# A seventh group by block products, and the residual added later: one transformer layer on one core

## The chip, the cores and the metric

The kernel runs on one core of a Trainium2 chip. The metric is device time in microseconds (us) for one execution. The core's engines each work through a queue of their own, in order: TensorE (PE; its weight loads stand apart as PEld), VectorE (DVE), ScalarE (ACT), GpSimd (POOL) and SyncE (SP). SP, POOL and ACT also issue transfers between device memory and the on-chip buffer (SBUF); matmul results land in eight PSUM banks.

## The reference

One decoder layer over 512 tokens with model width 2048, all in fp32:

```
h = x + gla_mixer(rmsnorm(x) * norm_mix) @ w_out          # gated linear attention, 4 heads
h = h + square(relu(rmsnorm(h) * norm_mlp @ w_up)) @ w_down   # 2048 -> 8192 -> 2048
gate = sigmoid(rmsnorm(h) * norm_ple @ w_ple_gate)        # 2048 -> 2048
h = h + gate * (p @ w_ple_proj)                           # p: 512 x 256
out = rmsnorm(h) * norm_final
```

The change lies in the product with `w_down`, in how the residual `h` is joined to it, and in the gate behind it.

## The kernel before, in words

Every matmul of weights is done three times: a helper splits each fp32 operand into a rounded high part and the low rest, and hi·hi, hi·lo and lo·hi are summed in PSUM (`mm3`, L148). ACT makes the high part, DVE the low part by a subtraction.

Activations lie transposed: 128 rows of features by 512 tokens. The token-wise scale of the MLP's norm is taken out of the matmuls. The hidden layer is computed from unscaled values; since relu squared of f·v is f²·relu²(v), the output of `w_down` lacks the factor F2 = f² of each token. So the residual is multiplied by 1/F2 (the tile `g2`) before the MLP's sum is added to it, and the whole by F2 at the end. Both factors are made in `rest_of_scale` (L818): a row of 4 values per partition is spread over a 128x512 tile by a matmul (`bcast`, L219).

`w_up` and `w_down` are worked in chunks: 512 rows of the weights by 256 columns. There are two ways for a chunk.

- *Block products* (`chunk`, L843). The 256x256 blocks with the two halves of the tokens form 2x2 block matrices, multiplied by seven products instead of eight (a Strassen scheme: `PRODUCTS`, L738). A chunk is 2 times 7 products times 3 = 42 matmuls of 256 columns. It needs sums of weight blocks, made by DVE in `chunk_sums` (L741: one instruction of 128x512, two of 128x256), two high parts of 128x896 on ACT (L846) and two low parts on DVE (L848); and sums of the activations' blocks (the operands `d`). At the end of a group of chunks `combine` (L860) adds the seven results from four PSUM banks into a tile `e` of the single buffer `w`, by one ACT copy and five DVE instructions.
- *Plain* (`plain_chunk`, L917): 24 matmuls of 512 columns, with one high part on ACT (L140) and one low part on DVE (L142), 128x1024 each. Two PSUM banks. There is nothing to combine.

The up product has 32 groups (g) of 4 chunks, all by block products. Its results go to device memory, as blocks (`z_d`) and as differences of blocks (`zd_d`). The down product has 8 groups of 256 output columns and 16 chunks of 512 rows, which are cut into five slices of 3, 3, 3, 3 and 4 chunks (`SLICES`, L34), since only a slice's hidden activations fit in SBUF. Within a slice all 8 groups run; groups in `PLAIN` = (0, 7) take the plain way, the other six block products. Slice 0 runs its groups in the order 0, 7, 1 to 6 (L761), the others in order.

After each group in each slice the partial result is added to the running residual: `residual_in` (L887) loads `h_d[g]` (512 KB), and in slice 0 multiplies it by `g2` (L891); DVE adds two times 128x512 (L903 or L927); `residual_out` (L894) writes it back, in slice 4 after a multiplication by F2 (L896). `late` work like this is queued in `todo` and run after the second chunk of the next group. While a slice runs, the hidden activations of the next are loaded and split (`build_to` and `build_sums_to`: `split`, L909, a POOL load, an ACT cast L913, a DVE subtraction L914, 128x1024 each), into 34 shared slots that come free as the old slice's chunks are used up.

Two smaller pieces lie between: `embedding` (L958) transposes `p`, in slice 0 after group 1; `project_embedding` (L971) multiplies it by a quarter of `w_ple_proj`, 24 matmuls of 512 columns into four PSUM banks, four ACT copies into two tiles, and two stores of 512 KB to `pp_d`; it follows group 7 in slices 1 to 3 and group 6 in slice 0. The gate stage behind (L1101) loads the finished residual, makes its squares' sums for the norm (`r3`, L1116), multiplies by `w_ple_gate` and ends in `finish` (L1091).

The order in which each engine's queue gets its instructions is made by a planner when the program is built: it goes through the program's order as priorities, with the times that it expects, and hands out buffers. An instruction whose data it expects later can be passed by others. At run time the queues are fixed.

Of the kernel before, what the change touches and what calls it, by code (L numbers as in the profile page):

```python
# [9 lines left out]
F32 = mybir.dt.float32  # L10
# [6 lines left out]
P = 128  # L17
# [16 lines left out]
SLICES = (3, 3, 3, 3, 4)  # L34
PLAIN = (0, 7)

# [24 lines left out]
def trunk_kernel(ctx, tc, a, out):  # L61
# [723 lines left out]
    def evac_out(i, ps):  # L785
        kp = i // 2
        if i % 2 == 0:
            late["x"] = (load2 if kp == 5 else load)([P, 2, T], f"xres_{kp}")
            nc.gpsimd.dma_start(late["x"], xT_d[i:i + 2].rearrange("k p t -> p k t"))
            if kp in (5, 6):  # L790
                late["u"] = late["x"]
            else:
                late["w"] = wide(f"u_{kp}")
                late["u"] = late["w"][:, 0:4, :].rearrange("p (a h) t -> p a (h t)", a=2)
            late[kp] = late["u"]
        h = late["x"][:, i % 2, :]
        nc.vector.tensor_tensor(out=h, in0=ps, in1=h, op=ALU.add)
        add_squares(h, f"mlp_{i}", i == 0)
        if kp not in (5, 6):
            scale_out(i, h)  # L800
        if i % 2:
            nc.gpsimd.dma_start(h_d[kp], late["x"])
            if kp in (5, 6):
                for j in range(2):
                    scale_out(i - 1 + j, late["x"][:, j, :])
            if i == 13:
                first_raw.append(raw_of(0))
            if kp < 5:
                XOPS[kp] = operands(kp, late["u"], late["w"][:, 4:8, :], "X")
# [4 lines left out]

    F2 = []
    g2 = mpool.tile([P, T], F32, tag="g2", name="g2")

    def rest_of_scale():  # L818
# [5 lines left out]
        nc.vector.tensor_tensor(out=f, in0=r, in1=rinv, op=ALU.mult)  # L824
        ft = tiny([P, NTT], "ft")
        nc.vector.tensor_tensor(out=ft, in0=f, in1=f, op=ALU.mult)
        F2.append(mpool.tile([P, T], F32, tag="acc2", name="f2"))
        bcast(ft, F2[0], "f2")
        gi_ = tiny([P, NTT], "gi")
# [56 lines left out]

    def residual_in(s_, g):  # L887
        hs = (load2 if g % 3 == 2 else load)([P, 2, T], f"h_{s_}_{g}")
        nc.gpsimd.dma_start(hs, h_d[g])
        if s_ == 0:  # L890
            nc.vector.tensor_tensor(out=hs, in0=hs, in1=g2.unsqueeze(1).broadcast_to([P, 2, T]), op=ALU.mult)  # L891
        return hs

    def residual_out(s_, g, hs):  # L894
        if s_ == len(SLICES) - 1:
            nc.vector.tensor_tensor(out=hs, in0=hs, in1=F2[0].unsqueeze(1).broadcast_to([P, 2, T]), op=ALU.mult)  # L896
        nc.gpsimd.dma_start(h_d[g], hs)

    def add_slice(s_, g, ps):
        _, z = combine(ps, f"dn{s_}_{g}")  # L900
        hs = residual_in(s_, g)
        for f in range(2):
            nc.vector.tensor_tensor(out=hs[:, f, :], in0=hs[:, f, :], in1=z[:, 1 - f, :], op=ALU.add)  # L903
        residual_out(s_, g, hs)

# [17 lines left out]

    def add_plain(s_, g, ps):
        hs = residual_in(s_, g)
        for i in range(2):
            nc.vector.tensor_tensor(out=hs[:, i, :], in0=hs[:, i, :], in1=ps[i], op=ALU.add)  # L927
        residual_out(s_, g, hs)
    built = [0, 0]
# [41 lines left out]
    def project_embedding(gi):  # L971
        hi, lo = load_w(w_rows(w_pp, 0, 2, 512 * gi, 512), [P, 2, 512], f"wp{gi}")
        for t2 in range(NTT // 2):
            o = (load2 if (2 * gi + t2) % 3 == 2 else load)([P, 2, 512], f"pp_{gi}_{t2}")
            for t in range(2):
                ts_ = slice((2 * t2 + t) * P, (2 * t2 + t + 1) * P)
                ps = bank(f"ps_ple{gi}_{t2}_{t}")
                for k in range(2):
                    mm3(ps, (PT[k][:, 0, ts_], PT[k][:, 1, ts_]), (hi[:, k, :], lo[:, k, :]), k == 0, k == 1)
                nc.scalar.copy(o[:, t, :], ps)  # L980
            nc.scalar.dma_start(
                pp_d[2 * t2:2 * t2 + 2, :, 512 * gi:512 * gi + 512].rearrange("t p c -> p t c"), o)

    raw_next = first_raw[0]
    ps = None
    for n, (stage, g, k4, first, last) in enumerate(work):
        raw, raw_next = raw_next, raw_of(n + 1)
        s_ = stage - 1
        if stage == 0:
# [6 lines left out]
            if g == 0 and k4 == 2:  # L996
                rest_of_scale()
        else:
            end = sum(SLICES[:stage])
            if g == 0:  # L1000
                build_to(k4 + 1)
# [3 lines left out]
            if g in PLAIN:  # L1005
                if first:
                    ps = [bank(f"ps_{name}_{i}") for i in range(2)]
                plain_chunk(ps, k4, g, first, last, f"{name}_{k4}")
                if s_ == 0 and g == 0:
                    flush()  # L1010
                    build_to(min(k4 + 2, end))
                if s_ == 0 and g == 7:
                    build_sums_to(k4 + 1)
            else:
                if first:
                    ps = group_banks(g % 2 == 0, name)
                chunk(ps, raw, k4, ZOPS, first, last, f"{name}_{k4}")
            if last and end < NG // 2:
                if g == 1 and not s_:
                    embedding()  # L1020
                if g == 2 and SLICES[s_] == 3:
                    build_to(end + 2)
                if g == 6:
                    build_to(end + 3)
                if g == (7 if s_ else 6):
                    project_embedding(s_)
                    build_sums_to(end + 1)
        if todo and not first:
            todo.pop(0)()
        if last:  # L1030
            if stage == 0:
                ze = []
                todo.append(lambda g=g, ps=ps, ze=ze: ze.append(hidden(g, ps)))
                todo.append(lambda g=g, ze=ze: hidden_sums(g, *ze))
            else:
                todo.append(lambda s_=s_, g=g, ps=ps: (add_plain if g in PLAIN else add_slice)(s_, g, ps))
    flush()
# [53 lines left out]
    def finish(t, gi, psg, pp, ph):  # L1091
# [4 lines left out]
        d = hn[t][c0 // 1024][:, c0 % 1024:c0 % 1024 + w]  # L1096
        nc.vector.tensor_tensor(out=d, in0=sg[:, :w], in1=ph, op=ALU.add)
        nc.scalar.activation(out=sg[:, :w], in_=d, func=AF.Square, accum_out=ssf[:, t, gi:gi + 1])
        nc.vector.tensor_tensor(out=d, in0=d, in1=nf[c0 // 1024][:, c0 % 1024:c0 % 1024 + w], op=ALU.mult)

    for gi, (c0, w) in enumerate(GROUPS):  # L1101
        nk = 1024 // w
        if gi < len(GROUPS) - 1:
# [61 lines left out]
```

## Time and profile before

| | |
|---|---|
| median of 3 runs | 2371.59 us (2369.11 to 2375.26) |
| the profiled execution | 2369.4 us, its span 2367.6 us |
| PE busy | 2331.3 us, 98% of the span |
| PEld busy | 2129.9 us, 90% |
| DVE busy | 1731.8 us, 73% |
| ACT busy | 987.2 us, 42% |
| POOL busy | 186.7 us, 8% |
| granted TensorE clock, mean | 0.997 |

The span runs from the first to the last instruction of the profiled execution. Shares are means over all stages: DVE's 73% hides that it is lighter in the gate and the mixer and heavier in the MLP. The down product lies between 1469.9 and 2170.2 us of the span, the gate stage behind it.

### The profile page before, as it was taken

The page shows a single profiled execution, that of the slowest core. Times are in us where ns is not written, and L with a number is a line of the kernel's source. Part 1 is how long each engine was busy: PE and PEld are TensorE (multiplying, and loading weights), DVE is VectorE, ACT ScalarE, POOL GpSimd, SP SyncE. Part 2 cuts the span into 40 slices and gives each one's busy share as a digit, 9 for nine tenths or more (in the row PEclk, how much of TensorE's full clock was granted, in tenths as well). Part 3 has the DMA queues.
Part 4 walks back from the last instruction along what each step waited for, and adds up shares of the span by engine and source line. Part 5 has one row for each costly group of instructions (what it writes and reads, how often), then busy time and mean ns, then how long its engine had stood idle before and what let it go on. Part 6 is the DMA issues. An engine that isn't in the chain of part 4 may idle for free.

```text
span 2367.6 us, 37470 instructions
## 1 busy us (share of the span) xinstructions
PE 2331.3 (98%) x15066; PEld 2129.9 (90%) x15066; DVE 1731.8 (73%) x2700; ACT 987.2 (42%) x1237; POOL 186.7 (8%) x346
## 2 busy tenths in 40 slices
PE   8999999999999999999999999999999999999998
PEld 7888888888888899999999999898989898998887
DVE  6664737447555698988898887798979687898435
ACT  5433323324333345444444444444443444335233
POOL 3000000000100000000000001101010101101000
PEclk9999999999999999999999999999999999999999
DMA  8322323232434345545554446647575757646433
GB/s 277 106 81 89 89 81 104 84 98 85 135 128 151 118 157 163 167 154 160 161 159 154 158 151 216 219 161 273 191 263 176 276 169 258 198 160 216 119 114 113
DMA packets 256975, 374.73 MB, mean 158 GB/s; under 512 B 14756, under 2 KB 203360, under 8 KB 256800
## 3 DMA queue, kind: packets, MB, share of 16 engines
q1 hardware_dynamic: 213072, 228.68, 31.6%
q0 software_dynamic: 39456, 139.31, 16.4%
q10 hardware_dynamic: 4272, 4.33, 0.6%
q8 instruction: 118, 1.93, 0.3%
q14 instruction: 57, 0.47, 0.1%
HBM read 297.83 MB, written 74.45 MB: 157 GB/s over the span
## 4 chain that ended last, share of the span: by engine, by line
PE 85%; DMA 5%; DVE 4%; issue 2%; ACT 1%; POOL 0%; ACTq 0%; DVEq 0%; POOLq 0%
PE ps_up L857 8%; PE ps_up L856 8%; PE ps_up L854 8%; PE ps_d L857 5%; PE ps_d L854 5%; PE ps_d L856 5%; PE ps_v L150 2%; PE ps_wo L150 2%; PE ps_wo L151 2%; PE ps_v L151 2%; PE ps_og L150 2%; PE ps_og L151 2%; PE ps_v L152 2%; PE ps_og L152 2%; PE ps_wo L152 2%
## 5 line engine op out<-in xcount | busy, mean ns | idle before, releaser
L846 ACT CAST whi_up<-raw_up 128x896 fp32r<-128x896 f32 x256 | 238.3, 940 | 299.0 <-PE ps_up L856 255.6
L848 DVE TENSOR_TENSOR wlo_up<-raw_up,whi_up 128x896 fp32r<-128x896 f32 x256 | 277.3, 1086 | 43.8 <-ACT whi_up L846 43.8
L854 PE MATMUL ps_up<-XS,whi_up 128*128 128x256 f32 x1024 | 290.1, 283 | 0.0
L857 PE MATMUL ps_up<-XS,wlo_up 128*128 128x256 f32 x1024 | 290.0, 283 | 0.0
L856 PE MATMUL ps_up<-XS,whi_up 128*128 128x256 f32 x1024 | 289.7, 283 | 0.0
L846 ACT CAST whi_d<-raw_dn 128x896 fp32r<-128x896 f32 x192 | 176.7, 942 | 259.4 <-DVE raw_dn L750 117.8
L857 PE MATMUL ps_up<-XA,wlo_up 128*128 128x256 f32 x768 | 218.1, 284 | 2.0 <-DVE wlo_up L848 1.9
L854 PE MATMUL ps_d<-Zdh,whi_d 128*128 128x256 f32 x768 | 217.8, 284 | 0.4 <-DVE e_dn L867 0.4
L854 PE MATMUL ps_up<-XA,whi_up 128*128 128x256 f32 x768 | 217.4, 283 | 0.4 <-ACT whi_up L846 0.4
L856 PE MATMUL ps_d<-Zdl,whi_d 128*128 128x256 f32 x768 | 217.7, 283 | 0.0
L857 PE MATMUL ps_d<-Zdh,wlo_d 128*128 128x256 f32 x768 | 217.4, 283 | 0.0
L856 PE MATMUL ps_up<-XA,whi_up 128*128 128x256 f32 x768 | 217.3, 283 | 0.0
L848 DVE TENSOR_TENSOR wlo_d<-raw_dn,whi_d 128x896 fp32r<-128x896 f32 x192 | 206.1, 1084 | 10.9 <-ACT whi_d L846 10.2
L854 PEld LDWEIGHTS ps_up<-XS,whi_up 128*128 128x128 f32 x1024 | 196.5, 192 | 0.2 <-issue 0.2
L856 PEld LDWEIGHTS ps_up<-XS,whi_up 128*128 128x128 f32 x1024 | 196.5, 192 | 0.2 <-issue 0.2
L857 PEld LDWEIGHTS ps_up<-XS,wlo_up 128*128 128x128 f32 x1024 | 196.5, 192 | 0.2 <-issue 0.2
L854 PE MATMUL ps_d<-Zuh,whi_d 128*128 128x256 f32 x576 | 163.4, 284 | 7.3 <-ACT whi_d L846 4.9
L857 PE MATMUL ps_d<-Zuh,wlo_d 128*128 128x256 f32 x576 | 163.8, 284 | 2.4 <-DVE wlo_d L848 2.4
L856 PE MATMUL ps_d<-Zul,whi_d 128*128 128x256 f32 x576 | 163.0, 283 | 0.0
L857 PEld LDWEIGHTS ps_up<-XA,wlo_up 128*128 128x128 f32 x768 | 147.4, 192 | 3.3 <-DVE wlo_up L848 3.2
L854 PEld LDWEIGHTS ps_d<-Zdh,whi_d 128*128 128x128 f32 x768 | 147.9, 193 | 0.5 <-issue 0.5
L854 PEld LDWEIGHTS ps_up<-XA,whi_up 128*128 128x128 f32 x768 | 147.4, 192 | 0.5 <-ACT whi_up L846 0.5
(345 smaller groups left out, 6011.6 us busy)
## 6 DMA issues: line engine op xcount, KB each, us to landing
raw_up<-in_w_up SPq DMA_DIRECT2D x128, 512.0 KB, 3.8
raw_dn<-in_w_down SPq DMA_DIRECT2D x96, 512.0 KB, 3.7
h<-h_d POOLq DMA_DIRECT2D x40, 512.0 KB, 4.9
h_d<-h POOLq DMA_DIRECT2D x40, 512.0 KB, 3.1
raw_v<-in_gla_w_in SPq DMA_DIRECT2D x32, 512.0 KB, 3.9
raw_og<-in_gla_w_in SPq DMA_DIRECT2D x32, 512.0 KB, 3.7
raw_wo<-in_gla_w_out SPq DMA_DIRECT2D x32, 512.0 KB, 3.4
z_d<-e_up POOLq DMA_DIRECT2D x64, 256.0 KB, 2.6
```

The source lines that it names most:

```text
L150: nc.tensor.matmul(ps, lhsT=wa[0], rhs=wb[0], start=first, stop=False)
L151: nc.tensor.matmul(ps, lhsT=wa[0], rhs=wb[1], start=False, stop=False)
L152: nc.tensor.matmul(ps, lhsT=wa[1], rhs=wb[0], start=False, stop=last)
L846: nc.scalar.copy(hi[:, 1:8, :], raw[:, q_, 1:8, :])
L848: nc.vector.tensor_tensor(out=lo[:, 1:8, :], in0=raw[:, q_, 1:8, :], in1=hi[:, 1:8, :].bitcast(F32), op=ALU.subtract)
L854: nc.tensor.matmul(dst, lhsT=hi[:, wb, :], rhs=xh, start=first and q_ == 0 and half == 0, stop=False)
L856: nc.tensor.matmul(dst, lhsT=hi[:, wb, :], rhs=xl, start=False, stop=False)
L857: nc.tensor.matmul(dst, lhsT=lo[:, wb, :], rhs=xh, start=False, stop=last and q_ == 1 and (b == 3 or half == 1))
```

## The change

`PLAIN` becomes (0,): group 7 takes block products too, in every slice, and slice 0 runs its groups in plain order. The partial sums start without the residual: slice 0 writes its results to `h_d`, and the residual, kept in `h0_d`, is loaded, multiplied by `g2` and added in slices 1 to 4, for two groups in each (slice 1 + g % 4). The loads of `h_d` are issued at a group's first chunk instead of in the late work. The factor F2 is not multiplied in any more; it stays a value per token (`ftok`) and goes into the gate's scale, the norm's sums and the last addition. `project_embedding` moves to the first chunk of group 0 in slices 1 to 4, and collects its quarter in one tile of the buffer `w`, stored by one transfer of 1 MB. `embedding` moves into group 3 of the up product.

```diff
-PLAIN = (0, 7)
+PLAIN = (0,)
...
-        for g in range(NKP) if s_ else (0, 7, 1, 2, 3, 4, 5, 6):
+        for g in range(NKP):
...
-            nc.gpsimd.dma_start(h_d[kp], late["x"])
+            nc.gpsimd.dma_start(h0_d[kp], late["x"])
...
-        ft = tiny([P, NTT], "ft")
-        nc.vector.tensor_tensor(out=ft, in0=f, in1=f, op=ALU.mult)
-        F2.append(mpool.tile([P, T], F32, tag="acc2", name="f2"))
-        bcast(ft, F2[0], "f2")
+        nc.vector.tensor_tensor(out=ftok, in0=f, in1=f, op=ALU.mult)
...
     def residual_in(s_, g):
+
         hs = (load2 if g % 3 == 2 else load)([P, 2, T], f"h_{s_}_{g}")
-        nc.gpsimd.dma_start(hs, h_d[g])
-        if s_ == 0:
-            nc.vector.tensor_tensor(out=hs, in0=hs, in1=g2.unsqueeze(1).broadcast_to([P, 2, T]), op=ALU.mult)
+        if s_:
+            nc.gpsimd.dma_start(hs, h_d[g])
         return hs
 
-    def residual_out(s_, g, hs):
-        if s_ == len(SLICES) - 1:
-            nc.vector.tensor_tensor(out=hs, in0=hs, in1=F2[0].unsqueeze(1).broadcast_to([P, 2, T]), op=ALU.mult)
+    def join_in(s_, g, hs):
+        if s_ == 1 + g % 4:
+            for k, tag in enumerate(("acc2", "d")):
+                x = mpool.tile([P, T], F32, tag=tag, name=f"h0_{g}_{k}")
+                nc.gpsimd.dma_start(x, h0_d[g, :, k, :])
+                nc.vector.tensor_tensor(out=x, in0=x, in1=g2, op=ALU.mult)
+                nc.vector.tensor_tensor(out=hs[:, k, :], in0=hs[:, k, :], in1=x, op=ALU.add)
+
+    def add_slice(s_, g, ps, hs):
+        _, z = combine(ps, f"dn{s_}_{g}")
+        if s_:
+            for f in range(2):
+                nc.vector.tensor_tensor(out=hs[:, f, :], in0=hs[:, f, :], in1=z[:, 1 - f, :], op=ALU.add)
+            join_in(s_, g, hs)
+            nc.gpsimd.dma_start(h_d[g], hs)
+        else:
+            for f in range(2):
+                nc.gpsimd.dma_start(h_d[g, :, f, :], z[:, 1 - f, :])
+
+    def add_plain(s_, g, ps, hs):
+        for i in range(2):
+            if s_:
+                nc.vector.tensor_tensor(out=hs[:, i, :], in0=hs[:, i, :], in1=ps[i], op=ALU.add)
+            else:
+                nc.scalar.copy(hs[:, i, :], ps[i])
+        join_in(s_, g, hs)
         nc.gpsimd.dma_start(h_d[g], hs)
...
-        for t2 in range(NTT // 2):
-            o = (load2 if (2 * gi + t2) % 3 == 2 else load)([P, 2, 512], f"pp_{gi}_{t2}")
...
+        o = wide(f"pp_{gi}").rearrange("p (a b) t -> p a (b t)", b=2)
+        for t in range(NTT):
...
+        nc.scalar.dma_start(pp_d[:, :, 512 * gi:512 * gi + 512].rearrange("t p c -> p t c"), o)
...
+            if g == 3 and k4 == 2:
+                embedding()
         else:
             end = sum(SLICES[:stage])
+            if first:
+                hs = residual_in(s_, g) if s_ or g in PLAIN else None
...
                 plain_chunk(ps, k4, g, first, last, f"{name}_{k4}")
+                if first and s_:
+                    project_embedding(s_ - 1)
                 if s_ == 0 and g == 0:
                     flush()
                     build_to(min(k4 + 2, end))
-                if s_ == 0 and g == 7:
-                    build_sums_to(k4 + 1)
+                    build_sums_to(k4)
             else:
                 if first:
-                    ps = group_banks(g % 2 == 0, name)
+                    ps = group_banks(g % 2, name)
...
-                if g == 1 and not s_:
-                    embedding()
...
-                if g == (7 if s_ else 6):
-                    project_embedding(s_)
+                if g == 7:
                     build_sums_to(end + 1)
...
-        nc.vector.tensor_tensor(out=d, in0=sg[:, :w], in1=ph, op=ALU.add)
+        nc.vector.scalar_tensor_tensor(
+            out=d, in0=ph, scalar=ftok[:, t:t + 1], in1=sg[:, :w], op0=ALU.mult, op1=ALU.add)
...
-                nc.vector.tensor_copy(r3, rstd_of(token_sums(acc2, "ple"), D, NTT, "ple"))
+                ssum = tiny([P, NTT], "ssum_ple")
+                nc.vector.tensor_tensor(out=ssum, in0=token_sums(acc2, "ple"), in1=ftok, op=ALU.mult)
+                nc.vector.tensor_tensor(out=ssum, in0=ssum, in1=ftok, op=ALU.mult)
+                nc.vector.tensor_tensor(out=r3, in0=rstd_of(ssum, D, NTT, "ple"), in1=ftok, op=ALU.mult)
```

## Rows read from the trace of the kernel before

**Rows 1.** The page's busy time, share of the span, instructions, for every engine.
```profile
PE 2331.3 (98%) x15066; PEld 2129.9 (90%) x15066; DVE 1731.8 (73%) x2700; ACT 987.2 (42%) x1237; POOL 186.7 (8%) x346
```

**Rows 2.** Five slices: from:to, length, busy PE PEld DVE ACT POOL, clock, DMA, GB/s.
```profile
1469.90:1606.60 136.70, 131.07 (x934) 123.39 (x933) 116.07 (x171) 58.17 (x68) 15.19 (x28) 1.00 0.61 206
1606.60:1740.50 133.90, 130.67 (x926) 123.36 (x924) 111.77 (x160) 59.75 (x69) 17.02 (x32) 0.99 0.70 241
1740.50:1871.30 130.80, 129.17 (x925) 122.18 (x924) 107.84 (x155) 55.56 (x66) 14.90 (x28) 1.00 0.64 219
1871.30:2004.20 132.90, 129.61 (x925) 122.28 (x924) 107.57 (x156) 56.16 (x67) 14.89 (x28) 1.00 0.63 213
2004.20:2170.20 166.00, 164.75 (x1201) 157.08 (x1201) 138.45 (x199) 70.11 (x86) 14.36 (x27) 1.00 0.60 201
```

**Rows 3.** Waits in 1469:2170: engine line, releaser, us in total, times, longest us.
```profile
DVE Zul L914 <- ACT Zuh L913: 27.4, 10, 5.2
DVE Zdl L914 <- ACT Zdh L913: 22.3, 7, 6.5
...
DVE wlo_d L142 <- ACT whi_d L140: 18.8, 9, 4.4
DVE raw_dn L746 <- DMA raw_dn<-in_w_down: 14.8, 13, 2.6
...
PE ps_d L150 <- ACT pp L980: 5.0, 3, 2.1
PE ps_d L854 <- ACT whi_d L846: 4.9, 3, 2.5
```

**Rows 4.** PE in order of time, slice 2: first and last matmuls of each kind.
```profile
1758.78 0.28 PE L854 MATMUL ps_d<-Zuh,whi_d 128*128 128x256 f32 x1
...
1849.38 0.28 PE L857 MATMUL ps_d<-Zuh,wlo_d 128*128 128x256 f32 x1
1849.49 0.40 PE L150 MATMUL ps_d<-Zuh,whi_d 128*128 128x512 f32 x1
...
1865.62 0.39 PE L152 MATMUL ps_d<-Zuh,wlo_d 128*128 128x512 f32 x1
```

**Rows 5.** DVE in order of time: start us, us, line, operation.
```profile
1588.96 0.41 DVE L865 TENSOR_TENSOR e_dn<-ps_d,e_dn 128x256 f32<-128x256 f32 x1
...
1591.40 1.08 DVE L848 TENSOR_TENSOR wlo_d<-raw_dn,whi_d 128x896 fp32r<-128x896 f32 x1
1592.40 1.28 DVE L903 TENSOR_TENSOR h<-h,e_dn 128x512 f32<-128x512 f32 x2
...
1747.16 0.68 DVE L746 TENSOR_TENSOR raw_dn<-raw_dn 128x512 f32<-128x512 f32 x1
...
1748.68 1.22 DVE L914 TENSOR_TENSOR Zul<-Zul,Zuh 128x1024 fp32r<-128x1024 f32 x1
1749.82 2.09 DVE L848 TENSOR_TENSOR wlo_d<-raw_dn,whi_d 128x896 fp32r<-128x896 f32 x2
```

**Rows 6.** A stretch of block products in slice 0; columns as in rows 2.
```profile
1521.10:1601.20 80.10, 76.84 (x630) 75.94 (x631) 75.29 (x114) 34.59 (x41) 8.51 (x16) 1.00 0.54 179
```

**Rows 7.** PE in order of time at two stops; in brackets idle time and releaser.
```profile
1521.12 0.39 PE L854 MATMUL ps_d<-Zuh,whi_d 128*128 128x256 f32 x1 [2.39 <-DVE e_dn L865]
...
1622.78 0.39 PE L152 MATMUL ps_d<-Zuh,wlo_d 128*128 128x512 f32 x1
1625.66 0.39 PE L854 MATMUL ps_d<-Zuh,whi_d 128*128 128x256 f32 x1 [2.49 <-ACT whi_d L846]
```

**Rows 8.** DVE in slice 0: a split of hidden differences that comes late.
```profile
1498.70 1.22 DVE L914 TENSOR_TENSOR Zdl<-Zdl,Zdh 128x1024 fp32r<-128x1024 f32 x1
```

**Rows 9.** PE in order of time: the spreading of the two factors in the up product.
```profile
835.71 1.12 PE L226 MATMUL ps_bc_f<-dg_f,ones 128*128 128x512 f32 x2
...
836.80 1.10 PE L226 MATMUL ps_bc_g<-dg_g,ones 128*128 128x512 f32 x2
```

**Rows 10.** DVE at the end of the gate's first group.
```profile
2214.77 0.16 DVE L197 TENSOR_SCALAR ms_ple<-ps_ts_ple 128x4 f32<-128x4 f32 x1 [3.91 <-PE ps_ts_ple L216]
```

More of the change, by code (lines that the diff above doesn't have):

```diff
@@ L123, in trunk_kernel @@
     gated_d = dram.tile([NK, P, T], F32, name="gated_d")
+    h0_d = dram.tile([NKP, P, 2, T], F32, name="h0_d")
     h_d = dram.tile([NKP, P, 2, T], F32, name="h_d")
@@ L812, in trunk_kernel @@
     proj_a(w_out, 0, GH, 0, D, evac_out, None, "wo")
-    F2 = []
+    ftok = rinv
     g2 = mpool.tile([P, T], F32, tag="g2", name="g2")
@@ L888, in residual_in @@
         hs = (load2 if g % 3 == 2 else load)([P, 2, T], f"h_{s_}_{g}")
-        nc.gpsimd.dma_start(hs, h_d[g])
-        if s_ == 0:
-            nc.vector.tensor_tensor(out=hs, in0=hs, in1=g2.unsqueeze(1).broadcast_to([P, 2, T]), op=ALU.mult)
-        return hs
-    def residual_out(s_, g, hs):
-        if s_ == len(SLICES) - 1:
-            nc.vector.tensor_tensor(out=hs, in0=hs, in1=F2[0].unsqueeze(1).broadcast_to([P, 2, T]), op=ALU.mult)
-        nc.gpsimd.dma_start(h_d[g], hs)
[L899 to L904, printed above, removed]
+        if s_:
+            nc.gpsimd.dma_start(hs, h_d[g])
+        return hs
+    def join_in(s_, g, hs):
[22 more added lines that the diff above has]
+        join_in(s_, g, hs)
+        nc.gpsimd.dma_start(h_d[g], hs)
     ZOPS = [None] * NG
@@ L922, in plain_chunk @@
                 mm3(ps[i], (hi[:, kk, s], lo[:, kk, s]), ZH[4 * k4 + kk], first and kk == 0, last and kk == 3)
[L924 to L928, printed above, removed]
     built = [0, 0]
@@ L972, in project_embedding @@
         hi, lo = load_w(w_rows(w_pp, 0, 2, 512 * gi, 512), [P, 2, 512], f"wp{gi}")
-        for t2 in range(NTT // 2):
-            o = (load2 if (2 * gi + t2) % 3 == 2 else load)([P, 2, 512], f"pp_{gi}_{t2}")
[L975 to L982, printed above, removed]
+        o = wide(f"pp_{gi}").rearrange("p (a b) t -> p a (b t)", b=2)
+        for t in range(NTT):
+            ts_ = slice(t * P, (t + 1) * P)
+            ps = bank(f"ps_ple{gi}_{t}")
+            for k in range(2):
+                mm3(ps, (PT[k][:, 0, ts_], PT[k][:, 1, ts_]), (hi[:, k, :], lo[:, k, :]), k == 0, k == 1)
+            nc.scalar.copy(o[:, t, :], ps)
+        nc.scalar.dma_start(pp_d[:, :, 512 * gi:512 * gi + 512].rearrange("t p c -> p t c"), o)
     raw_next = first_raw[0]
@@ L1035, in trunk_kernel @@
             else:
-                todo.append(lambda s_=s_, g=g, ps=ps: (add_plain if g in PLAIN else add_slice)(s_, g, ps))
+                todo.append(lambda s_=s_, g=g, ps=ps, hs=hs: (add_plain if g in PLAIN else add_slice)(s_, g, ps, hs))
     flush()
```

## The prediction

> **What bounds the kernel now.** I read the page's busy times first: TensorE works 98% of the span [rows 1]. Then the five slices of the down product, where nearly all of the change lies [rows 2]. They last 136.7, 133.9, 130.8, 132.9 and 166.0 us, together 700.3 us; PE is busy almost throughout, at a granted clock of 0.99 to 1.00 (the 2.4 GHz level), and VectorE for 116.1, 111.8, 107.8, 107.6 and 138.5 us, between 81% and 85%. So PE is the bound and DVE is the next one. The table of waits [rows 3] tells which kind of stop there is: PE waits little and for single late things (ACT's copies of `pp`, ACT's high parts), while DVE's waits on casts and on weights are 27.4 + 22.3 + 18.8 + 14.8 = 83.3 us over five slices, 16.7 a slice, today hidden behind PE.
>
> How much of the 700.3 us is matmul time? Matmuls overlap, so their step is read from starts. 756 matmuls of block products start between 1758.78 and 1849.38, 755 steps of 0.120 us; 72 plain ones between 1849.49 and 1865.62, 71 steps of 0.227 us [rows 4]. A chunk by block products is thus 42 x 0.120 = 5.04 us of PE, a plain one 24 x 0.227 = 5.45 us. Before: 96 chunks at 5.04, 32 at 5.45, and four quarters of the embedding, each again 24 matmuls of 512 columns, 5.45: 680.0 us, and about 1 us of transposes. So PE stands still for some 19 us in the whole down product.
>
> **The change part by part.**
>
> *Group 7, PE.* 16 chunks go from 5.45 to 5.04: 6.6 us less. The down product needs 112 x 5.04 + 16 x 5.45 + 4 x 5.45 = 673.5 us (the transposes move into the up product and cost there what they cost here). By slice: 122.2 without the embedding, 127.6 three times, 168.4; the embedding's quarter leaves slice 0 and comes into slice 4.
>
> The steps per column are 0.469 and 0.443 ns: short matmuls cost more per column, and only one product of eight saved outweighs it. The Trainium skill speaks against short ones too ("Perfetto Trace Analysis", Matmuls: larger matmuls are more efficient), but its figure for a warm step (columns at 2.4 GHz plus about 2.5 ns; "TensorE: Matmul & The Clock Gate", Wait — 56ns, not 53.3ns?) would make the steps 0.109 and 0.216 us and the saving 16 x (5.18 - 4.59) = 9.5 us. The rows measure 0.120 and 0.227 in this kernel, so 6.6 us stands.
>
> *Group 7, DVE.* Steps again from starts [rows 5]: the weights' sums take 1748.68 - 1747.16 = 1.52 us; two low parts 2 x (1592.40 - 1591.40) = 2.00; a 128x1024 subtraction 1749.82 - 1748.68 = 1.14; a combine 1591.40 - 1588.96 = 2.44; two additions of 128x512 1.28. So a chunk by block products is 3.52 us of DVE, a plain one 1.14. Group 7 adds 3 x 2.38 + 2.44 = 9.6 us of DVE to a slice, 12.0 in slice 4.
>
> *Residual and factor, DVE.* Slice 0 loses eight multiplications by g2 (8 x 1.14 = 9.1) and 16 additions (8 x 1.28 = 10.2). Slices 1 to 4 get two joins each, a join being two multiplications and two additions of 128x512: 2 x 1.28 = 2.56, so 5.1 a slice. Slice 4 loses F2: 9.1. Late work of a slice's last group runs in the next slice, so 1.14 + 1.28 = 2.4 of slice 0's lies in slice 1's window. DVE after: slice 0 116.1 + 9.6 - 19.3 - 2.4 (the embedding's two subtractions of 128x512 and one of 128x1024) = 104; slice 1 111.8 + 9.6 + 5.1 - 2.4 = 124.1; slices 2 and 3 122.5 and 122.3; slice 4 138.5 + 12.0 + 5.1 - 9.1 = 146.5. Against PE's 127.6 that is 96 to 97% in slices 1 to 3, and 87% or less in slices 0 and 4.
>
> *What such a load costs.* Bounds: nothing, if DVE never waits while PE needs it (127.6 a slice); at the other end all DVE idle time of today stays, 22.1, 23.0 and 25.3 us [rows 2], 439 us for the three. The nearest row is the stretch of slice 0 in which DVE is already that full: 75.3 of 80.1 us, 94%, with PE at 76.8 [rows 6]. I take 94%: 132.0 + 130.3 + 130.1 = 392.4 us for slices 1 to 3 (397.6 before, 5.2 less).
>
> *Slice 0.* PE 122.2. The stop after the transposes of `p`, 2.4 us for a combine [rows 7], goes with them. Late next: block products now begin after one plain group, at 1469.9 + 16.3 = 1486.2, and the second half of their third chunk, at 1498.8, needs a split that today starts at 1498.70 and ends 1.1 later [rows 8]: 1.0 late. In the same time DVE has two chunks of group 1 to prepare (2 x 3.52) where it had two plain ones (2 x 1.14), 4.8 more. Bounds: 0, if the load goes out earlier, and 5.8; I take 3, next to the 2.4 that a late DVE cost at this place [rows 7]: 125.2, 11.5 less than before.
>
> *Slice 4.* PE 168.4, DVE far below. Its start has the turn from slice to slice (next); between 0 and the 5.0 there I take 2.5: 170.9, 4.9 more than before, since the embedding's quarter came in. The last group's residual is ready 2.44 + 1.28 + 2.56 us of DVE and two transfers behind its last matmul; the gate first needs it after 14 of the 16 steps of its first group, 14 x 12 x 0.227 = 38 us: nothing.
>
> *The turn.* Group 7 now holds differences of the old slice to its end, so the next slice's come 16 us later and have group 0 and the embedding, 21.8 us of PE, to be loaded and split. Before, only the turn from slice 0 to 1 was like that, and slice 1, whose matmuls need 18 x 5.04 + 7 x 5.45 = 128.9 us, took 133.9 [rows 2]: 5.0 lost, of which 2.7 in one stop at its first block products, from 1622.78 to 1625.66 less a step [rows 7]. Also the embedding's tile is now the combine's buffer, so group 7's combine can stand in ACT's queue until the 1 MB store has landed, with casts behind it. In favour: `h_d` loads no longer wait in POOL's queue for late work, and the 5.0 us that PE waited for the `pp` copies [rows 3] goes, as group 0 has its banks before. For slices 1 to 3 this is inside the 94%.
>
> *Small edits.* One spreading matmul pair less: 836.80 - 835.71 = 1.1 us [rows 9] (0 if PE waits for the second one anyway). Two more tiny operations before `r3`, 0.16 us each and a gap [rows 10], and a slower form of the last addition: 0 to 1, I take 0.5. POOL gets some 15 more issues in 700 us; it is busy 76 of them. The earlier loads of `h_d` I cost at nothing: they are issued a group ahead, 15 us, of the additions that use them; without that lead each would cost DVE a wait.
>
> **The sum.** -11.5 - 5.2 + 4.9 - 1.1 + 0.5 = -12.4 us on the profiled execution's own 2369.4 (1.8 of which lie outside its span and stay): 2357.0. That execution lies 2.2 us below the median of the runs; for a median I go part of the way and predict 2358.
>
> **The rivals.**
>
> *All stops vanish.* 673.5 instead of 700.3, less 0.6: 2342. For it: slice 2 today runs its 756 block-product matmuls without a stop [rows 4]. Against: DVE at 96%.
>
> *Every turn costs what the turn from 0 to 1 costs today*, 5.0 us, and nothing is lost elsewhere: 125.2 + 3 x 132.6 + 173.4 = 696.4, 3.9 less, with the small edits 2365. For it: the same sequence of groups. Against: loads of `h_d` no longer stand in POOL's queue ahead of the splits' loads.
>
> *DVE becomes the bound (slower).* DVE's queue is in order; in slices 1 to 3 its 16.7 us of waits on casts and weights [rows 3] no longer hide if look-ahead never fills: 368.9 + 3 x 16.7 = 419.0, 21.4 more than before. With -11.5, +4.9 and -0.6 that is 14.2 us more: 2384. It decides above 12.0 us of waits a slice, where the total is zero. For it: a group of three chunks needs 3 x 3.52 + 3.72 = 14.3 us of DVE against 15.1 of PE, so a join (2.6) or split (1.14) is not made up within a group. Against: rows 6, where waits were 4.8 us in 80, some 8 a slice. The Trainium skill says that ScalarE and VectorE are strict first-in first-out while TensorE may pull weight loads ahead ("TensorE: Matmul & The Clock Gate", Architectural detail); the stop of 2.4 us behind DVE's combine [rows 7] agrees.
>
> **How the numbers follow.** The forecast, 2350 to 2364, has 0.46; no stops, 2341 to 2350, 0.09; the costly turns, 2364 to 2377, 0.26; DVE as bound, above 2377, 0.19. A measurement of this kernel tells about 0.3% from no change, 7 us: faster is below 2364.5, slower above 2378.7. Faster 0.55, same 0.28 (the turns and a little of the last), slower 0.17. The range, 2344 to 2386, leaves out half of the no-stop case and the end of the last, whose bound with all idle time kept is 2404.
>
> **What would show it.** Each step: PE's stretch from first to last down matmul about 689 us; DVE busy 94% in slices 1 to 3 and about 104 us in slice 0; no stop behind the embedding for `pp` copies. Wrong: waits of PE for L848 or L846 spread over groups 1 to 7 (DVE as bound), or one stop of several us at group 1 of each slice, behind a combine that waits for the `pp_d` store.

## The result, and the profile after

The changed kernel takes 2453.78 us (median of 4 runs, 2452.3 to 2459.24) against 2372.51 us for the kernel before: the ratio is 1.0349, with an interval of 1.0335 to 1.0363. It is slower by about 81 us, where the forecast was some 14 us faster (2358) and the range ended at 2386. The profiled execution took 2453.3 us, its span 2451.5 us.

The page's busy times of the changed kernel stand against [rows 1]:

```profile
PE 2346.8 (96%) x15352; PEld 2157.0 (88%) x15352; DVE 1774.9 (72%) x2790; ACT 1005.6 (41%) x1259; POOL 195.0 (8%) x361
```

The five slices of the down product after, cut at each slice's first matmul (from:to, length, busy PE PEld DVE ACT POOL, clock, DMA share, GB/s), against [rows 2]:

```profile
1470.80:1611.70 140.90, 127.56 (x957) 122.81 (x956) 111.93 (x165) 62.14 (x73) 19.33 (x36) 0.95 0.57 194
1611.70:1762.10 150.40, 132.61 (x981) 127.04 (x980) 119.35 (x178) 58.56 (x69) 17.13 (x32) 0.94 0.58 194
1762.10:1917.80 155.70, 133.00 (x980) 127.45 (x979) 122.71 (x182) 59.40 (x71) 17.08 (x32) 0.93 0.58 197
1917.80:2074.50 156.70, 135.74 (x981) 130.03 (x980) 121.59 (x181) 58.90 (x70) 17.07 (x32) 0.92 0.57 193
2074.50:2252.10 177.60, 171.56 (x1299) 165.69 (x1298) 143.56 (x213) 71.12 (x84) 13.86 (x26) 0.97 0.56 190
```

The down product takes 781.3 us, against 700.3 before: all of the loss but 2.9 us lies here. DVE has done what was worked out for it (619.1 us), yet it is busy only 78 to 81% of each slice. The granted clock has fallen to 0.92 to 0.97 in every slice.

PE's waits in the same stretch (engine, line, releaser, us, times, longest), against [rows 3]:

```profile
PE ps_d L851 <- ACT whi_d L843: 51.9, 9, 12.6
PE ps_ple L151 <- ACT pp L987: 25.0, 4, 7.4
PE ps_d L854 <- DVE wlo_d L845: 3.8, 7, 1.1
```

Where do the 781.3 us go? I took the starts of all matmuls in order of time and compared each step with 0.120 us (256 columns) or 0.227 us (512): 673.5 us are the matmuls' need as predicted; 70.5 us lie in eight stops of over 5 us, two at each turn from slice to slice; 20.8 us in 167 steps that are 0.07 to 0.24 us too long, nearly all right behind a stop; 16.3 us in small stops. Before, the same count gives 680.0 + 0 + 2.6 + 17.0. So the change did save its 6.6 us of PE, and lost 70.5 + 18.2.

Between the stops all is well. Three windows of slice 1: its groups 1 to 7 up to the first stop, that stop, and the second one:

```profile
1643.50:1739.50 96.00, 95.94 (x797) 95.74 (x798) 89.57 (x143) 36.20 (x43) 10.19 (x19) 1.00 0.57 184
1739.50:1762.00 22.50, 12.01 (x87) 11.74 (x86) 12.63 (x13) 10.30 (x11) 4.78 (x9) 0.77 0.67 229
1762.00:1782.20 20.20, 12.79 (x51) 10.12 (x51) 8.45 (x9) 7.61 (x10) 1.06 (x2) 0.83 0.70 256
```

For 96 us PE runs without a stop with DVE busy 93% of them. Then PE is busy for 58% of the next 43 us.

**Stop A, inside group 7** (9.7, 10.8, 11.9 and 12.9 us in slices 0 to 3). The timeline of slice 1, all engines, unconcerned rows left out (start us, us, engine, line, operation; in brackets idle time and releaser):

```profile
1737.22 0.53 POOL L925 DMA_DIRECT2D Zul<-z_d  x1 [6.83 <-PE ps_d L853]
...
1738.43 0.53 POOL L925 DMA_DIRECT2D Zul<-z_d  x1
...
1742.69 1.23 DVE L927 TENSOR_TENSOR Zul<-Zul,Zuh 128x1024 fp32r<-128x1024 f32 x1 [5.34 <-ACT Zuh L926]
1743.16 0.54 POOL L888 DMA_DIRECT2D h<-h_d  x1 [4.21 <-DMA h_d<-h]
1743.76 1.12 POOL L925 DMA_DIRECT2D Zdl<-zd_d  x2
1744.35 1.04 ACT L926 CAST Zuh<-Zul 128x1024 fp32r<-128x1024 f32 x1 [1.69 <-DMA Zul<-z_d]
1745.43 1.23 DVE L927 TENSOR_TENSOR Zul<-Zul,Zuh 128x1024 fp32r<-128x1024 f32 x1 [1.51 <-ACT Zuh L926]
1746.57 0.68 DVE L747 TENSOR_TENSOR raw_dn<-raw_dn 128x512 f32<-128x512 f32 x1
...
1748.37 1.04 ACT L926 CAST Zdh<-Zdl 128x1024 fp32r<-128x1024 f32 x1 [2.97 <-DMA Zdl<-zd_d]
1749.32 1.78 ACT L843 CAST whi_d<-raw_dn 128x896 fp32r<-128x896 f32 x2
...
1750.30 0.58 PE L851 MATMUL ps_d<-Zuh,whi_d 128*128 128x256 f32 x1 [10.49 <-ACT whi_d L843]
```

Read from below: PE waits for the high parts of group 7's next chunk (L843), whose casts stand behind a cast for the next slice; the sums of that chunk's weights (L747) stand in DVE's queue behind two splits of the next slice (L927), and the loads of those splits were issued only when a matmul of group 7 had given up its slot (POOL waited 6.83 us for `ps_d L853`). So group 7 waits for the next slice's data, and these wait for group 7's own first chunk. `chunk_sums` pins its first addition in program order (the planner may not move it ahead of DVE instructions that the program gave before it), and the program asks for the next slice's third chunk at group 6's end, ahead of it. While group 7 was plain it had no sums to pin.

**Stop B, in the embedding's quarter** (6.3, 7.8, 6.1 and 6.4 us), and **stop C, at group 1** (1.8, 3.1 and 2.7 us in slices 1 to 3). ACT behind slice 0:

```profile
1622.44 1.04 ACT L141 CAST whi_d<-raw_d 128x1024 fp32r<-128x1024 f32 x1 [9.07 <-DMA raw_d<-in_w_down]
1623.39 1.99 ACT L926 CAST Zdh<-Zdl 128x1024 fp32r<-128x1024 f32 x2
1625.28 1.06 ACT L987 COPY pp<-ps_ple 128x512 f32<-128x512 f32 x2
...
1631.88 0.38 ACTq L988 DMA_DIRECT2D pp_d<-pp  x1
...
1636.05 0.37 ACT L861 COPY e_dn<-ps_d 128x256 f32<-128x256 f32 x1 [2.70 <-DMA pp_d<-pp]
```

PE filled two banks by 1619.65 and could go on only at 1625.91, behind the first copy; the copies stood behind a cast that waited 9.07 us for its weights. Group 7's combine (L861) started 24 us after its last matmul (1611.57), since its buffer held the embedding's tile until the 1 MB store had landed; until then group 7 held its four banks. Stop C is the tail of this: the sums of group 1's weights stood in DVE's queue right behind the combine's instructions (L747 at 1638.91), and group 1's first matmul came at 1643.54.

PE at stop A of slice 0, around its return:

```profile
1590.21 0.28 PE L854 MATMUL ps_d<-Zuh,wlo_d 128*128 128x256 f32 x1
1599.93 0.58 PE L851 MATMUL ps_d<-Zuh,whi_d 128*128 128x256 f32 x1 [9.43 <-ACT whi_d L843]
1600.31 0.42 PE L853 MATMUL ps_d<-Zul,whi_d 128*128 128x256 f32 x1
1600.52 0.42 PE L851 MATMUL ps_d<-Zdh,whi_d 128*128 128x256 f32 x1
```

A window right behind this stop (columns as in the slices):

```profile
1599.90:1602.40 2.50, 2.47 (x11) 2.48 (x12) 2.50 (x4) 2.50 (x4) 0.00 (x0) 0.50 0.00 0
```

After the stop a step of 256 columns takes 0.21 us instead of 0.12, and the granted clock is 0.50: the 1.2 GHz level, half of full speed. The Trainium skill says that the clock is throttled unless activity releases it ("TensorE: Matmul & The Clock Gate", What's actually happening); the granted 0.50 behind PE's 9.43 us of standing still agrees.

### The profile page after: what moved, and what is told of

Same layout as the page of the kernel before. It is cut to its first block, busy times and chain, and to the rows that moved or that the text cites. A ratio compares the mean times of both kernels' runs of the same rounds, so it can differ in the third digit from the quotient of the medians.

```text
span 2451.5 us, 38202 instructions
## 1 busy us (share of the span) xinstructions
PE 2346.8 (96%) x15352; PEld 2157.0 (88%) x15352; DVE 1774.9 (72%) x2790; ACT 1005.6 (41%) x1259; POOL 195.0 (8%) x361
## 4 chain that ended last, share of the span: by engine, by line
PE 77%; issue 9%; DMA 7%; DVE 4%; ACT 2%; POOL 1%; SPq 0%; ACTq 0%; POOLq 0%; DVEq 0%
PE ps_up L854 8%; PE ps_up L853 8%; PE ps_up L851 8%; PE ps_d L854 6%; PE ps_d L851 6%; PE ps_d L853 6%; DMA raw_d<-in_w_down 3%; PE ps_v L151 2%; PE ps_wo L151 2%; PE ps_wo L152 2%; PE ps_og L153 2%; PE ps_v L153 2%; PE ps_og L152 2%; PE ps_v L152 2%; PE ps_og L151 2%
## 5 line engine op out<-in xcount | busy, mean ns | idle before, releaser
L843 ACT CAST whi_up<-raw_up 128x896 fp32r<-128x896 f32 x256 | 239.9, 940 | 319.0 <-PE ps_up L853 288.8
L843 ACT CAST whi_d<-raw_dn 128x896 fp32r<-128x896 f32 x224 | 206.8, 941 | 307.3 <-PE ps_d L853 166.7
L853 PE MATMUL ps_up<-XS,whi_up 128*128 128x256 f32 x1024 | 291.2, 284 | 0.0
L845 DVE TENSOR_TENSOR wlo_d<-raw_dn,whi_d 128x896 fp32r<-128x896 f32 x224 | 241.7, 1088 | 25.7 <-ACT whi_d L843 24.4
L851 PE MATMUL ps_d<-Zdh,whi_d 128*128 128x256 f32 x896 | 257.1, 287 | 0.0
L853 PE MATMUL ps_d<-Zdl,whi_d 128*128 128x256 f32 x896 | 256.8, 287 | 0.0
L854 PE MATMUL ps_d<-Zdh,wlo_d 128*128 128x256 f32 x896 | 255.4, 287 | 0.0
L851 PE MATMUL ps_d<-Zuh,whi_d 128*128 128x256 f32 x672 | 193.6, 288 | 51.9 <-ACT whi_d L843 51.9
L853 PE MATMUL ps_up<-XA,whi_up 128*128 128x256 f32 x768 | 217.8, 284 | 0.0
L854 PE MATMUL ps_d<-Zuh,wlo_d 128*128 128x256 f32 x672 | 194.2, 289 | 3.8 <-DVE wlo_d L845 3.8
L853 PEld LDWEIGHTS ps_up<-XS,whi_up 128*128 128x128 f32 x1024 | 197.2, 193 | 0.2 <-issue 0.2
L853 PE MATMUL ps_d<-Zul,whi_d 128*128 128x256 f32 x672 | 192.5, 287 | 0.0
L851 PEld LDWEIGHTS ps_d<-Zuh,whi_d 128*128 128x128 f32 x672 | 131.0, 195 | 54.7 <-ACT whi_d L843 54.6
L853 PEld LDWEIGHTS ps_d<-Zdl,whi_d 128*128 128x128 f32 x896 | 175.5, 196 | 0.0
```

Source lines behind the costliest of these rows:

```text
L843: nc.scalar.copy(hi[:, 1:8, :], raw[:, q_, 1:8, :])
L845: nc.vector.tensor_tensor(out=lo[:, 1:8, :], in0=raw[:, q_, 1:8, :], in1=hi[:, 1:8, :].bitcast(F32), op=ALU.subtract)
L851: nc.tensor.matmul(dst, lhsT=hi[:, wb, :], rhs=xh, start=first and q_ == 0 and half == 0, stop=False)
L853: nc.tensor.matmul(dst, lhsT=hi[:, wb, :], rhs=xl, start=False, stop=False)
L854: nc.tensor.matmul(dst, lhsT=lo[:, wb, :], rhs=xh, start=False, stop=last and q_ == 1 and (b == 3 or half == 1))
```

## The experiments

Every edit makes the planner order the whole program anew, so differences of a few us between two kernels are not put down to a part. Behind each time stands its ratio to the kernel before, run beside it, with a 95% interval.

**Which part makes stop A?** First the pin, then the place of the early splits, then group 7 plain, then group 7 alone put into the kernel before.

```diff
# e1_no_pin: in chunk_sums
-        tc.keep_in_program_order(nc.vector.tensor_tensor(...))
+        nc.vector.tensor_tensor(...)
# e12_unpin_down: in chunk_sums
+        if name.startswith("up"):
+            tc.keep_in_program_order(add)
# e2_late_build
-                if g == 6:
-                    build_to(end + 3)
                 if g == 7:
+                    build_to(end + 3)
                     build_sums_to(end + 1)
# e3_plain7
-PLAIN = (0,)
+PLAIN = (0, 7)
# e4_only_g7: the kernel before with this, and with slice 0's order,
# the banks, the split sums and the quarter behind group 7 that go with it
-PLAIN = (0, 7)
+PLAIN = (0,)
...
```

> Edit: the weights' sums of a chunk (L747 of the changed kernel) are no longer pinned behind DVE's instruction that the program traced before them; nothing else. Theory P (the stop inside group 7 comes from that pin: the sums of group 7's second chunk stand in DVE's queue behind a split whose slots come free only by group 7's own first chunk): the four stops of 9.7, 10.8, 11.9 and 12.9 us inside group 7 go, with the half clock behind them some 50 us in all; the stops in the embedding (6 to 8 us each) and at group 1 stay at least in part: 2395 to 2412 us. Rival L (DVE's load with group 7 by block products, or loads that land late and hold ACT's in-order queue whatever the pin): the stops stay, 2440 to 2460. Rival R (the moved embedding and the residual's edits are the cause): no change, 2445 to 2460.

Measured: 2446.93 us, 1.0309 (1.0284 to 1.0335). Stop A is gone, the gain is not: without the pin the up product takes longer too (the down product starts at 1500.66 instead of 1470.8), and the waits of stop B grow to 39.9 us. The run is confounded; e12 frees the down product alone.

> The kernel after with the sums of the weights pinned in the program's order for the up product only, free in the down product (e1_no_pin freed both, and lost 30 us in the up product). My theory: stop A (PE's 52 us of waits for group 7's high parts) goes, the up product is as in after, stop B grows somewhat as in e1 (40 us of waits on the pp copies against 25): 2453.8 - 45 + 10 = 2418, 2405 to 2430. Rival, the pin is not the cause of A but only e1's other order was: above 2440.

Measured: 2412.82 us, 1.0171 (1.0153 to 1.0189). PE's waits in its down product:

```profile
PE ps_ple L151 <- ACT pp L989: 39.9, 4, 14.2
PE ps_d L856 <- DVE wlo_d L847: 11.7, 14, 2.3
PE ps_d L853 <- ACT whi_d L845: 0.9, 1, 0.9
```

The wait for high parts fell from 51.9 to 0.9 us and the time by 41 us, with the up product as it was.

> Edit: the splits of the next slice's third chunk (two loads, casts and subtractions) are traced behind group 7 instead of behind group 6; the pin stays. Theory P: the sums of group 7's chunks have no such split in front of them any more, the four stops inside group 7 go, 2395 to 2412 us; the turn behind it may get a little fuller, since the same splits now all lie there. Rival L: the splits still wait for the same slots and land late, DVE has the same work: 2440 to 2460. Rival R: 2445 to 2460.

Measured: 2405.68 us, 1.0143 (1.0125 to 1.0161); PE's waits:

```profile
PE ps_ple L151 <- ACT pp L987: 29.6, 4, 12.8
PE ps_d L851 <- ACT whi_d L843: 9.4, 5, 2.7
```

With the pin kept but the splits asked for later, stop A goes as well, for 48 us (the waits for high parts that are left are 2.7 us at most). So it takes both: a pinned instruction, and a slot-limited load ahead of it in the program.

> Edit: the changed kernel with group 7 plain again (PLAIN = (0, 7)); residual, factor and embedding stay as changed. Theory P: a plain group 7 makes no sums, so nothing of it can stand behind the splits: the stops inside group 7 go; the embedding's stops behind late weights shrink too, since the differences' slots come free 16 us earlier; PE works 6.6 us more: 2375 to 2405 us. Rival L says about the same, 2365 to 2385. Rival R: the loss stays, 2440 to 2465.

Measured: 2403.21 us, 1.0126 (1.0103 to 1.0148). No stop A with group 7 plain. But this edit does more than its text says: the embedding's quarter hangs on the first chunk of a plain group, so in slices 1 to 4 it is worked twice, in group 0 and in group 7. The trace has 192 of its matmuls instead of 96, and 32 copies instead of 16:

```profile
L987 ACT COPY pp<-ps_ple x32: 567/587/595, 1608.1 to 2207.9; 128x512 f32<-128x512 f32 x32
```

96 matmuls too many are 96 x 0.227 = 21.8 us of PE, and PE waits 16.0 us around the eight quarters. So the run shows that stop A goes, and its time says nothing of a plain group 7; e10 below does.

> Edit: the kernel before with group 7 by block products alone (groups in plain order in every slice, the embedding's quarter behind group 7, the same bank order as changed); residual and factor as before. Theory P: the splits are traced behind group 6 here too, so the four stops inside group 7 of some 10 to 13 us appear, with 6.6 us of PE saved and the slow clock paid: 2405 to 2425 us. Rival L: DVE has also the two multiplications and additions in the wrong slices: 2430 to 2460. Rival R: group 7 is harmless, 2360 to 2370.

Measured: 2429.34 us, 1.0237 (1.0214 to 1.0259); PE's waits there:

```profile
PE ps_d L854 <- ACT whi_d L846: 50.2, 7, 11.3
PE ps_d L150 <- ACT pp L980: 7.2, 3, 3.4
```

Group 7 by block products, with the order that goes with it and nothing else of the change, brings stop A into the kernel before (10.4 to 11.5 us in slices 0 to 3) and costs 57 us: stop A needs neither the residual's new place nor the factor's. Here the `pp` copies cost 7.2 us, not 25.0, so B belongs to the embedding's new form or place.

**Which part makes stops B and C?** The embedding's place moved, with and without stop A, and its tiles alone put back.

```diff
# e5_late_mid: as e2_late_build, and (e7_mid_only: this part alone)
-                if first and s_:
-                    project_embedding(s_ - 1)
...
+        if s_ > 0 and g == 5 and k4 == end - SLICES[s_] + 1:
+            project_embedding(s_ - 1)
# e6_late_old_tiles: as e2_late_build, and in project_embedding
-        o = wide(f"pp_{gi}")...
+            o = (load2 if (2 * gi + t2) % 3 == 2 else load)([P, 2, 512], f"pp_{gi}_{t2}")
```

> The kernel after with only the embedding's quarter moved to the middle chunk of group 5; the third chunk's loads stay at group 6's end. My theory: stop A stays as it is (PE's wait on the high parts of group 7, about 50 us over four slices), stops B and C go: 2453.8 less some 40 = 2414, 2405 to 2422. Rival, the stops at group 0 are made by the burst of slot loads and not by the embedding: PE then waits there for other things and the time stays above 2440.

Measured: 2409.05 us, 1.0159 (1.0136 to 1.0181). B and C are gone, A is left (46.8 us of waits for high parts).

> As e2_late_build, but the embedding's quarter is collected in two tiles outside the combine's buffer and stored by two transfers of 512 KB, as before the change; its place in group 0 stays. My theory: stop C (the sums of group 1 behind a combine that waits for the store, 1.0 to 3.1 us a slice) goes, stop B (waits on the pp copies, 29.6 us) stays, for it has its cause in the two free PSUM banks and the copies' place in ACT's queue: 2396, 2390 to 2402. Rival, the 1 MB tile in the combine's buffer is the cause of both: 2367. Rival, the tile doesn't matter at all: 2405.

Measured: 2384.95 us, 1.006 (1.0038 to 1.0083). My theory was wrong in one point: B goes too, all four quarters run without a stop in the very place where they stopped. PE's waits and ACT's combine behind slice 0 in this kernel:

```profile
PE ps_d L851 <- ACT whi_d L843: 14.9, 7, 5.4
PE ps_d L854 <- DVE wlo_d L845: 11.4, 17, 1.2
```

```profile
1603.08 1.05 ACT L926 CAST Zdh<-Zdl 128x1024 fp32r<-128x1024 f32 x1
1604.03 0.36 ACT L861 COPY e_dn<-ps_d 128x256 f32<-128x256 f32 x1
...
1607.85 0.57 ACT L988 COPY pp<-ps_ple 128x512 f32<-128x512 f32 x1
...
1622.77 1.07 ACT L988 COPY pp<-ps_ple 128x512 f32<-128x512 f32 x2 [4.40 <-DMA pp_d<-pp]
```

Group 7's combine runs ahead of the first `pp` copy now, 4.5 us after the group's last matmul instead of 24, and gives its banks to the embedding. Late copies matter only if the banks run out: the last two come 12 us behind the quarter's last matmul (1610.36), and PE doesn't stop. So B comes from the buffer `w` shared with the combine. C goes as the wait behind the combine, but group 1 isn't free of stops: inside it, before its second or third chunk is done, PE now waits 2.1, 2.7, 2.5 and 5.5 us in slices 1 to 4, where ACT's high parts stand behind casts of the next operands whose loads came late (ACT waited 6.48 us for `zd_d` ahead of the longest). The Trainium skill speaks for the large transfer ("DMA: Bandwidth & Descriptors", Bandwidth: batch to 1 MiB and more), and the 1 MB store did land in 4.2 us. Two of 512 KB from tiles of their own are nevertheless 21 us better here; the size and the buffer were changed together, and the trace shows the buffer at work.

> The kernel after, with the loads of the next slice's third chunk asked for at group 7's end (as in e2_late_build), and with the embedding's quarter moved from group 0's first chunk to the middle chunk of group 5 in slices 1 to 4, where four PSUM banks are free and no burst of slot loads runs. My theory (stop A: group 7's own slots and the pinned sums; stop B: two free banks and ACT's copies behind late weights; stop C: group 7's combine behind the 1 MB store): all three stops go; from e2's 2405.7 the 29.6 us of waits on the pp copies and some 9 us of lead gaps go: 2367, between 2360 and 2375. Rival, DVE's load as the bound: DVE has the same work and PE stops elsewhere: 2395 to 2405. Rival, the embedding stops PE wherever it stands, by its own casts and copies: 2385 to 2405 with the wait on the pp copies now in group 5.

Measured: 2375.51 us, 1.0023 (1.0012 to 1.0034), 30 us below e2. The three stops together account for 78 of the 81 us: without them the changed kernel stands 0.2% above the one before. It doesn't beat it: counted as above, 31 us of its 704.5 us are small stops and long steps, most of them in groups 1 to 4 behind each turn, where PE waits for low parts and DVE for weights:

```profile
PE ps_d L854 <- DVE wlo_d L845: 12.3, 17, 1.4
DVE raw_dn L747 <- DMA raw_dn<-in_w_down: 30.7, 22, 4.6
DVE wlo_d L845 <- ACT whi_d L843: 22.8, 23, 4.9
```

**Is it DVE's load?** The joins left out, in the kernel after (e8) and in e5 (e9).

```diff
# e8_no_join, and on top of e5_late_mid: e9_late_mid_no_join
-        if s_ == 1 + g % 4:
+        if s_ > len(SLICES):
```

> The kernel after without the residual's joins: the residual of the attention is not added (the 16 loads, 16 multiplications and 16 additions of 128x512 are left out), 20.5 us of DVE less over slices 1 to 4, 5.1 a slice. DVE's load as the bound: the time falls by about as much, to 2433. My theory: the stops don't come from DVE's load, the time stays between 2447 and 2456.

Measured: 2449.36 us, 1.0332 (1.0302 to 1.0362). 20.5 us of DVE less gave some 4 us, and the two intervals overlap.

> As e5_late_mid, but without the residual's joins (the attention's residual is not added: 5.1 us of DVE a slice less in slices 1 to 4, 20.5 together). In e5 the big stops are gone, and some 31 us of small ones are left inside the block products (PE waits for low parts and high parts of weights, DVE 88 to 90% busy in slices 1 to 3 of 131 to 139 us). My theory: these small stops come from DVE's load, they shrink by about what DVE is relieved of: 2358, 2350 to 2364. Rival, they come from weights that land late (DVE waits 30.7 us for raw_dn), whatever DVE's load: 2370 to 2376.

Measured: 2374.11 us, 1.0015 (1.0002 to 1.0027), the same as e5. My theory of DVE's load fell for 5.1 us a slice (a second plain group takes off 9.6); the wait for weights stayed:

```profile
DVE raw_dn L747 <- DMA raw_dn<-in_w_down: 35.7, 24, 4.8
DVE wlo_d L845 <- ACT whi_d L843: 28.0, 27, 4.8
```

Why the weights land late stays open. Their loads stood in SP's queue until DVE's low parts had given buffers back (in e5 72 waits, 371.2 us together; in e10 below 61 waits, 313.3 us), so they aren't independent of DVE either.

**What is left, then?** The idea: plain groups are the time in which the next slice's splits and the weights' look-ahead are made. Three kernels change how many there are and where.

```diff
# e10_late_mid_plain7: as e5_late_mid, and
-PLAIN = (0,)
+PLAIN = (0, 7)
# e13_plain01: as e5_late_mid, and
-PLAIN = (0,)
+PLAIN = (0, 1)
# e14_plain7_order: as e10_late_mid_plain7, and
-        for g in range(NKP):
+        for g in range(NKP) if s_ else (0, 7, 1, 2, 3, 4, 5, 6):
```

> As e5_late_mid, but with group 7 plain as before the change: all of the change except its seventh group of block products, and without the stops at the turn. PE's need rises by 6.6 us, DVE's falls by 9.6 us a slice. If DVE's load makes the small stops, they nearly vanish and the time is below e5 and before: 2360, 2354 to 2366. Rival, the small stops are not DVE's: the 6.6 us of PE come on top of e5: 2382.

Measured: 2357.85 us, 0.9945 (0.993 to 0.9961): the best version, below both kernels. Its slices 1 to 3, each cut at group 1's start:

```profile
1616.80:1745.70 128.90, 128.90 (x926) 122.31 (x925) 109.74 (x161) 54.78 (x64) 17.08 (x32) 1.00 0.68 226
1745.70:1874.50 128.80, 128.80 (x926) 122.20 (x925) 111.44 (x163) 54.76 (x63) 17.06 (x32) 1.00 0.68 231
1874.50:2008.90 134.40, 134.40 (x950) 126.77 (x949) 115.75 (x166) 60.31 (x70) 17.05 (x32) 1.00 0.69 236
```

PE is busy the whole time; what is left of stops (7 us, against 19.6 before by the same count) is in slice 0.

> As e5_late_mid, but groups 0 and 1 are plain (32.5 us) and group 7 stays in block products, so the old slice's difference slots come free only at the slice's end. If the length of the plain stretch is what e5 lacks, the small stops go as in e10: 2358, 2354 to 2363, below before. If it is group 7's hold on the slots, they stay: 2372 to 2382.

Measured: 2358.68 us, 0.9955 (0.994 to 0.997), as good, though group 7 is in block products and holds its slots to the slice's end; its stops are 10 us together, against 31 in e5. So group 7's hold on the slots isn't what was left. What e10 and e13 share is a plain stretch of 32 us instead of 16 ahead of a slice's block products.

> As e10_late_mid_plain7, but slice 0 runs its groups in the order 0, 7, 1 to 6 as before the change, so 32.5 us of plain work stand ahead of its first block products. In e10 slice 0 lost 7.5 us at its first block products (waits for the high and low parts of weights behind late splits); these go: 2351, 2348 to 2355. Rival: as in before, the slots of group 6's block products then come free late at the turn to slice 1, and the stops move there: 2357 to 2361.

Measured: 2364.17 us, 0.9976 (0.9966 to 0.9986), 6 us above e10: the rival was right in kind (its range ended at 2361), stops came into slice 1 (8 us), and slice 0 kept one of 2.4. Slice 1 has two plain groups here as in e10, and DVE's lighter load with them, but only one of them ahead of its block products. So the number of plain groups doesn't do it; the length of the stretch ahead fits all three runs in the main (e10's 7 us, too, lie in slice 0, which has 16 us of plain work ahead). A kernel with two plain groups apart in every slice was not run.

**Is the embedding's place worth anything by itself?**

```diff
# e11_before_mid: the kernel before with
-                    project_embedding(s_)
...
+        if s_ > 0 and g == 4 and k4 == end - SLICES[s_] + 1:
+            project_embedding(s_ - 1)
```

> The kernel before with one thing of the change in another form: the embedding's quarter in the middle chunk of group 4 in slices 1 to 4 instead of behind group 7 (group 6 in slice 0), tiles and stores as before. The waits on the pp copies (5.0 us in the trace of before) go: 2365, 2360 to 2368. Rival, what stops PE at the turn are the splits, and it waits there as long for them: 2369 or above.

Measured: 2367.54 us, 0.9992 (0.9981 to 1.0002): no difference that can be told.

## Why the prediction was wrong

**What bounds the kernel** and **group 7, PE** held. The steps after are 0.120 and 0.227 us, as in [rows 4], and the need of 673.5 us is what the count above leaves when stops are taken out.

**Group 7, DVE** and **residual and factor, DVE** held: predicted 104 + 124.1 + 122.5 + 122.3 + 146.5 = 619.4 us, measured 619.1. The split between slices held less well: 111.9, 119.4, 122.7, 121.6 and 143.6, so 7.9 more than predicted in slice 0, 4.7 and 2.9 less in slices 1 and 4.

**What such a load costs** gave 392.4 us for slices 1 to 3, from the 94% of [rows 6]; they took 462.8, 70.4 more. Not because of the load: of the 80.0 us beyond PE's need of 382.8, 54.7 lie in stops A and B and 14.2 in the long steps. The other 11.0, with 6.9 of stop C in them, are near the 9.6 that the 94% stood for, though that is partly luck, since stop C has another cause. The text had put the turn of these slices "inside the 94%", and there it wasn't. DVE's load was not what set them: block products ran 96 us without a stop at 93%, and taking 20.5 us of it away changed nothing (e9, without the big stops). The rival *DVE becomes the bound* named the right side with the wrong mechanism; its waits of high and low parts spread over groups 1 to 7 aren't there.

**The turn** is the step that failed. It said that group 7 holds its slots to its end, and then asked only when the next slice's splits would be *needed*, at group 1. What the trace shows is that they were *queued* earlier, inside group 7, ahead of its own pinned sums: 9.7 to 12.9 us a turn, priced at nothing; the largest price in the text was 5.0 for a turn. It also said that the combine could stand behind the 1 MB store, gave that no price of its own, and in the next sentence let the 5.0 us of `pp` waits [rows 3] go, "as group 0 has its banks before". The first cancels the second: a combine that waits holds the banks, and the waits became 25.0 us. The text's own list of what would show it wrong had stop C, the smallest of the three.

In favour of the change it said that `h_d` loads no longer wait in POOL's queue. One did at stop A, 4.21 us for a store out of an `h` tile, with loads of splits behind it; what that adds to stop A was not measured apart.

**Slice 0**, 125.2 us predicted, took 140.9: its stop A with the long steps behind it is the larger part of that, the start of its block products the rest. **Slice 4**, 170.9 predicted, took 177.6, with a stop B of 6.4 us at its start instead of 2.5. Outside the down product the kernel is 2.9 us longer, where 0.6 less was expected; that was not followed up. Together 15.7 + 70.4 + 6.7 + 3.5 = 96.3 us, the whole distance from 2357.0 to the profiled 2453.3.

**All stops vanish** was worth 2342. The nearest that the runs came to it is e10 at 2358, with group 7 plain. Group 7 by block products can save 6.6 us of PE at most, and with one plain group a slice it gave back more in both pairs that set it apart: 57 us net (e4 against before), 18 us net (e5 against e10).

That the residual's new place is free is shown in part: e8 and e9 bound the joins' price at about 4 us. What the residual and the factor save by themselves was not measured alone. Nor is it shown which part makes e10 12 us faster than the kernel before; it isn't the embedding's place by itself (e11).

## What to carry to other kernels

Before turning a unit of work into another kind, list what it did for its neighbours: the plain group's 5.45 us a chunk were also, as e10 and e13 suggest, the time in which the next slice's operands and the weights' look-ahead were made. For each instruction that the new kind adds, ask what stands ahead of it in an in-order queue, and whether that waits for a buffer that only the instruction's own group gives back. A buffer shared by two uses ties their whole chains together, transfer and PSUM banks included, so price it by the last release and not by the copy that fills it.

## What was not expected of the hardware

A stop costs more than its length: behind the eight stops of 5.9 to 12.8 us (beyond a step) the matmul steps stayed long (0.21 us for 0.12, 0.43 for 0.23), 20.8 us in the down product against 2.6 before, about 0.3 us for each us of stop. And VectorE at 93% busy, in order, with a mean of 0.6 us an instruction, held up no matmul for 96 us.
